# A hybrid encoder block on one core: the triangular inverses of two groups of heads computed together on 128 lanes, their operands brought to lanes through DRAM, and the filler work laid out anew

## The chip, the cores and the metric

The kernel runs on one core of a Trainium2 chip. The core has TensorE (PE, matrix products, results in PSUM), VectorE (DVE), ScalarE (ACT), GpSimd (POOL) and SyncE (SP), each working through its own list of instructions in order, and 16 DMA engines that all queues share. In this kernel SP issues the loads of weights and POOL nearly all other transfers. The metric is the device time of one execution in microseconds; a version's figure is the median of several executions.

## What is computed

The reference is one layer of a streaming encoder: 512 tokens, width 1024, everything float32. After an RMS norm one wide projection feeds three token mixers (a short gated convolution, a gated linear recurrence, and RWKV-7 time mixing), which are gated and summed; an output projection, a second norm, a squared-ReLU MLP with 4096 hidden units and a last norm follow. The part that matters here is the RWKV-7 mixing, with 16 heads of width 64:

```python
def step(state, inp):
    r_t, w_t, k_t, v_t, kk_t, a_t = inp
    sa = einsum('bhvk,bhk->bhv', state, -kk_t)
    state = (state * w_t[:, :, None, :]
             + sa[..., None] * (kk_t * a_t)[:, :, None, :]
             + v_t[..., None] * k_t[:, :, None, :])
    y_t = einsum('bhvk,bhk->bhv', state, r_t)
```

The kernel doesn't step through tokens. It takes chunks of 64 tokens (8 chunks). Inside a chunk the dependence of tokens on earlier ones is a strictly upper triangular 64x64 matrix A for each head and chunk, and (1 - A) has to be inverted: 16 heads x 8 chunks = 128 inverses of 64x64. Each is made of two 32x32 diagonal blocks, inverted by substitution, and of one off-diagonal block, which is a product of three 32x32 matrices: the first inverse, A's off-diagonal block, the second inverse.

## The kernel before

**Projections.** All large matrix products run in three passes: a float32 weight is loaded by SP (`raw`, two buffers), split into a high and a low half (`whi` by ScalarE in line 146, `wlo` by VectorE through the helper of line 103; three buffers each), and lines 167 to 169 multiply high x high, high x low and low x high. One projection (`proj`, line 306) is one weight of 128x1024, 8 slices x 3 matmuls, into one of three PSUM banks (`pp`); it yields after every second slice, so in four pieces. A bank is free again when ScalarE or VectorE has copied it out.

**Groups.** The 16 heads are four groups of four. For each group g:

- `krv(g)` (line 418) projects keys, receptances and values of the group and forms with many VectorE operations the scaled operands AR and BK. It has 26 yields (20 for group 0).
- `amat(g)` (line 517) multiplies them to the matrices A (and others) for all eight chunks, masks them into the tile AX (tag AXt, one buffer) in lines 529 and 530, and stores parts of it (axd) and the transposed BK (bkd) in DRAM for later. Three yields.
- `inverse(g)` (line 546) inverts the group's 32 matrices. Each of the 64 diagonal 32x32 blocks gets a lane of its own: two VectorE transposes (line 553) bring the blocks from AX to `la` in lanes 64 to 127 of the tile Z, identities come from an input `eyes` into `xt`, and 31 steps of substitution follow, two VectorE operations each (lines 562 and 567, both recorded under line 103), on 64 lanes. Two transposes (line 575) bring the result back to matrix form TT, a third (line 580) makes a transposed copy d1 of the first blocks. Then 32 matmuls pG (line 587), a ScalarE copy, 32 matmuls pT (line 597) and another copy make the off-diagonal blocks, reading AX itself as one operand. One DMA stores the finished TT in DRAM (ttd, line 600).

**Chain.** When all inverses are there, `chain` (line 628) goes through the eight chunks with the state carried from one to the next: each chunk loads its pieces of vtd, axd, ttd, rtd and bkd (line 608, all on POOL's queue) and runs four rounds of small matmuls. Layer output, MLP and the final norm follow.

**What sets the order.** The work is written as Python generators. `ab(q)` (line 744), for eight q, is the work of the other two mixers: seven projections and some 30 vector operations, in 29 yields; all eight in a row are the filler `fl`, 232 yields. `weave(crit, fill, r, base)` (line 823) advances the critical generator and gives the filler r steps for each of its yields; what the critical one issues goes into the planner with a priority offset (the value that it yielded, or `base`). The planner orders each engine's list by priority; `pin` (line 171) keeps small matmuls together, and `keep_in_program_order` keeps an instruction where it was written. The outer order is in lines 859 to 866:

```python
    weave(krv(0, GS[0]), fl, R0)
    for g in range(NG):
        if g:
            fgr = fill_group(g)
            weave(inverse(g - 1, GS[g - 1]), fgr, R1, CPV)
            drain(fgr)
        weave(amat(g, GS[g]), fl, 1.0)
    weave(inverse(NG - 1, GS[NG - 1]), fl, R2, CPV)
```

`fill_group(g)` (line 842) is itself a mix: F_INV = 30 filler steps, then `krv(g)` with F_KRV = 9 filler steps for each N_KRV = 22 of its yields, then F_GAP = 3. So an inverse of one group is woven with filler and with the next group's krv. N_TT = 2 and NINV = 12 are the empty yields in `inverse` around the transposes and between d1 and pG: they only let filler in. An inverse has 59 yields. Beside the chain the rest of the filler runs, then `gate(q)` (line 726) for eight q, then the first part of the output projection (`fill_chain`, line 880, at R3 = 1.6 steps for each yield of the chain).

Of the kernel before, what the change touches and what calls it, by code (L numbers as in the profile page):

```python
# [9 lines left out]
F32 = mybir.dt.float32  # L10
# [14 lines left out]
N_TT, NINV, NG_T, N_LOAD = 2, 12, 4, 6  # L25


N_KRV = 22
F_INV, F_KRV, F_GAP = 30, 9, 3
# [68 lines left out]
def block_kernel(ctx, tc, xt, win, par, mulr, sw, wout, w1, w2, fg, cst, eyes, out):  # L98
# [418 lines left out]
    def amat(g, G_):  # L517

        G_.AX = p1.tile([P, 2, NC, 4, L], F32, tag="AXt", name="AXt")
        for c4 in range(2):  # L520
# [10 lines left out]
            yield  # L531
        gp.dma_start(axd[:, 0:64, g, 1].rearrange("c s e t -> s c (e t)"),
# [13 lines left out]
    def inverse(g, G_):  # L546
        AXt = G_.AX
        Z = p1.tile([P, 2, 32, 32], F32, tag="Z", name="Z")
        la, xt = Z[64:128, 0], Z[64:128, 1]
        dg = p1.tile([P, 32, 32], F32, tag="dg", name="dg")  # L550
        tmp = dg[64:128].rearrange("p a b -> p (a b)")
        for b in range(2):
            v.transpose(la[32 * b:32 * b + 32].rearrange("l s t -> l t s"),
                        AXt[32 * b:32 * b + 32, 0, :, :, 32 * b:32 * b + 32].rearrange("s c e t -> s t (c e)"))
        gp.dma_start(xt.rearrange("l s t -> l (s t)"), eyes)

        yield
        yield
# [10 lines left out]
        TT = Z[0:64].rearrange("p a b c -> p (a b c)").rearrange("p (l t) -> p l t", t=L)  # L569
        gp.memset(TT[32:64, :, 0:32], 0.0)  # L570
        for b in range(2):
            for _ in range(N_TT):
                yield CPI
            tc.keep_in_program_order(
                v.transpose(TT[32 * b:32 * b + 32, :, 32 * b:32 * b + 32].rearrange("s l t -> s t l"),
                            xt[32 * b:32 * b + 32].rearrange("l s t -> l t s")))
# [3 lines left out]
        tc.keep_in_program_order(v.transpose(d1[0:32], TT[0:32, :, 0:32]))  # L580
        for _ in range(NINV):
            yield CPI
        for half in range(2):
            pg = pm.tile([P, 16, 32], F32, tag="pm", name="pG")
            for i in range(16):
                l = 16 * half + i
                pin(i, lambda: pe.matmul(pg[32:64, i], AXt[0:32, 0, l // 4, l % 4, 32:64], d1[0:32, l],  # L587
                                             start=True, stop=True))
            ac.copy(gs[32:64, 16 * half:16 * half + 16], pg[32:64])
# [3 lines left out]
        for half in range(2):  # L593
            pg = pm.tile([P, 16, 32], F32, tag="pm", name="pT")
            for i in range(16):
                l = 16 * half + i
                pin(i + half, lambda: pe.matmul(pg[0:32, i], gs[32:64, l], TT[32:64, l, 32:64], start=True, stop=True))
            ac.copy(TT[0:32, 16 * half:16 * half + 16, 32:64], pg[0:32])
# [9 lines left out]
    def load_chunk(c):  # L608
# [9 lines left out]
        gp.dma_start(flat(tc_), flat(ttd[c]))  # L618
# [223 lines left out]
    def fill_group(g):  # L842

        for _ in range(F_INV):
            next(fl, None)
            yield
        acc = 0.0
        for _ in krv(g, GS[g]):
            yield
            acc += F_KRV / N_KRV  # L850
# [4 lines left out]
        for _ in range(F_GAP):  # L855
# [275 lines left out]
```

## Time and profile before

| | us |
|---|---|
| median of 3 executions | 1103.43 (1099.84 to 1107.11) |
| the profiled execution | 1100.19 |
| its span, first to last instruction | 1098.4 |
| PE busy | 1053.0 (96%) |
| DVE busy | 735.3 (67%) |
| ACT busy | 486.4 (44%) |
| POOL busy | 93.7 (9%) |

The four amat stages begin at about 87, 204, 327 and 450 us; the chain's first matmuls run at 564 us, its last at 669 us; the MLP takes the time from about 750 us to the end. In the profile a line such as L103 or L106 is that of a helper, so groups of one kind are told apart by the names of tiles and by shape (dg and Z for the inverse's steps). "Idle before" is the time that an engine stood still ahead of an instruction, with the instruction that ended it. The granted clock is the share of its full rate at which TensorE ran.

### The profile page before, as it was taken

The page shows a single profiled execution, that of the slowest core. Times are in us where ns is not written, and L with a number is a line of the kernel's source. Part 1 is how long each engine was busy: PE and PEld are TensorE (multiplying, and loading weights), DVE is VectorE, ACT ScalarE, POOL GpSimd, SP SyncE. Part 2 cuts the span into 40 slices and gives each one's busy share as a digit, 9 for nine tenths or more (in the row PEclk, how much of TensorE's full clock was granted, in tenths as well). Part 3 has the DMA queues.
Part 4 walks back from the last instruction along what each step waited for, and adds up shares of the span by engine and source line. Part 5 has one row for each costly group of instructions (what it writes and reads, how often), then busy time and mean ns, then how long its engine had stood idle before and what let it go on. Part 6 is the DMA issues. An engine that isn't in the chain of part 4 may idle for free.

```text
span 1098.4 us, 16103 instructions
## 1 busy us (share of the span) xinstructions
PE 1053.0 (96%) x6396; PEld 863.2 (79%) x6396; DVE 735.3 (67%) x1266; ACT 486.4 (44%) x718; POOL 93.7 (9%) x159
## 2 busy tenths in 40 slices
PE   8999989999999979999699998999999999999996
PEld 5777867787877867788578886998888888888885
DVE  7998987899788987889547777855444443222224
ACT  7755455444573545363445444334444443111114
POOL 0011001110111002200031210101000000000001
PEclk9999989999999989999799999999999999999999
DMA  6336324452446224453288753334332335333232
GB/s 219 120 95 183 100 81 131 130 158 87 138 127 172 82 85 123 123 159 105 70 265 256 252 196 104 116 111 158 96 96 96 96 96 192 96 96 96 95 97 76
DMA packets 43323, 142.13 MB, mean 129 GB/s; under 512 B 5680, under 2 KB 9264, under 8 KB 42224
## 3 DMA queue, kind: packets, MB, share of 16 engines
q1 hardware_dynamic: 29472, 91.02, 25.9%
q0 software_dynamic: 13056, 49.03, 14.8%
q8 instruction: 50, 0.82, 0.3%
q10 hardware_dynamic: 720, 1.05, 0.3%
q14 instruction: 25, 0.20, 0.1%
HBM read 115.91 MB, written 25.17 MB: 128 GB/s over the span
## 4 chain that ended last, share of the span: by engine, by line
PE 47%; DVE 2%; ACT 1%; issue 1%; DMA 0%; DVEq 0%; ACTq 0%
PE acc L167 7%; PE acc L168 7%; PE acc L169 7%; PE p L168 5%; PE p L169 5%; PE p L167 5%; PE pp L167 2%; PE pp L169 2%; PE pp L168 2%; PE py L654 1%; PE pu L644 1%; PE pu L664 1%; PE pS L673 1%; PE pG L587 0%; DVE xr L106 0%
## 5 line engine op out<-in xcount | busy, mean ns | idle before, releaser
L103 DVE TENSOR_TENSOR wlo<-raw,whi 128x1024 fp32r<-128x1024 f32 (+1 forms) x164 | 197.9, 1208 | 228.5 <-ACT whi L146 222.7
L146 ACT CAST whi<-raw 128x1024 fp32r<-128x1024 f32 (+1 forms) x164 | 169.6, 1035 | 274.7 <-PE acc L169 125.0
L167 PE MATMUL pp<-hh,whi 128*128 128x512 f32 x688 | 275.1, 400 | 7.2 <-ACT g L799 4.2
L169 PE MATMUL pp<-hh,wlo 128*128 128x512 f32 x688 | 273.4, 397 | 2.7 <-DVE wlo L103 2.7
L168 PE MATMUL pp<-hl,whi 128*128 128x512 f32 x688 | 273.6, 398 | 0.0
L167 PEld LDWEIGHTS pp<-hh,whi 128*128 128x128 f32 x688 | 131.2, 191 | 37.0 <-ACT g L799 4.8
L169 PEld LDWEIGHTS pp<-hh,wlo 128*128 128x128 f32 x688 | 131.2, 191 | 32.3 <-DVE wlo L103 4.8
L168 PEld LDWEIGHTS pp<-hl,whi 128*128 128x128 f32 x688 | 131.3, 191 | 27.0
L167 PE MATMUL p<-h2h,whi 128*128 128x512 f32 (+1 forms) x264 | 101.4, 384 | 0.0
L168 PE MATMUL p<-h2l,whi 128*128 128x512 f32 (+1 forms) x264 | 101.2, 383 | 0.0
L169 PE MATMUL p<-h2h,wlo 128*128 128x512 f32 (+1 forms) x264 | 101.1, 383 | 0.0
L167 PE MATMUL acc<-whi,ah 128*128 128x512 f32 x256 | 99.6, 389 | 0.0
L168 PE MATMUL acc<-wlo,ah 128*128 128x512 f32 x256 | 99.6, 389 | 0.0
L169 PE MATMUL acc<-whi,al 128*128 128x512 f32 x256 | 99.6, 389 | 0.0
L167 PEld LDWEIGHTS p<-h2h,whi 128*128 128x128 f32 x264 | 49.6, 188 | 9.7
L168 PEld LDWEIGHTS p<-h2l,whi 128*128 128x128 f32 x264 | 49.7, 188 | 9.5
L169 PEld LDWEIGHTS p<-h2h,wlo 128*128 128x128 f32 x264 | 49.6, 188 | 9.6
L169 PEld LDWEIGHTS acc<-whi,al 128*128 128x128 f32 x256 | 48.0, 188 | 10.1
L167 PEld LDWEIGHTS acc<-whi,ah 128*128 128x128 f32 x256 | 48.0, 188 | 10.0
L168 PEld LDWEIGHTS acc<-wlo,ah 128*128 128x128 f32 x256 | 48.0, 188 | 9.9
L103 DVE TENSOR_TENSOR dg<-Z 64x31 f32<-64x31 f32 (+15 forms) x124 | 42.2, 340 | 4.1
L103 DVE TENSOR_TENSOR Z<-Z,dg 64x31 f32<-64x31 f32 (+15 forms) x124 | 42.2, 340 | 4.1
(304 smaller groups left out, 1465.7 us busy)
## 6 DMA issues: line engine op xcount, KB each, us to landing
raw<-in_win SPq DMA_DIRECT2D x88, 512.0 KB, 3.5
raw<-in_w SPq DMA_DIRECT2D x64, 512.0 KB, 3.5
ax<-axd POOLq DMA_DIRECT2D x8, 1024.0 KB, 7.5
axd<-AXt POOLq DMA_DIRECT2D x12, 512.0 KB, 7.1
bkd<-BKT POOLq DMA_DIRECT2D x4, 1024.0 KB, 12.4
raw<-in_wout SPq DMA_DIRECT2D x8, 512.0 KB, 3.6
bk<-bkd POOLq DMA_DIRECT2D x7, 512.0 KB, 8.5
swr<-in_sw SPq DMA_DIRECT2D x16, 128.0 KB, 2.3
```

The lines of the kernel that those rows point to most:

```text
L103: return v.tensor_tensor(out=o, in0=a, in1=b, op=op)
L146: ac.copy(hi[:, sl], raw[:, sl])
L167: pe.matmul(ps, wh, xh, start=start, stop=False)
L168: pe.matmul(ps, wh, xl, start=False, stop=False)
L169: pe.matmul(ps, wl, xh, start=False, stop=stop)
L644: pin(n, lambda: pe.matmul(pu[64 * h:64 * h + 64, x], ax[rows, g, 0, e], sv[rows, g, e], start=True, stop=True))
L654: pin(behind, lambda: pe.matmul(py[64 * h:64 * h + 64, x], w, y, start=first and x == 0, stop=last, skip_group_check=True))
L664: pin(n, lambda: pe.matmul(pu[64 * h:64 * h + 64, x], tc_[:, g, e], u0[:, g, e], start=True, stop=True))
L673: pin(n, lambda: pe.matmul(pS[64 * h:64 * h + 64, x], bk[:, x, 64 * h:64 * h + 64], sv[:, g, e], start=True, stop=True))
```

## The change

Groups 0 and 1 are inverted together, and groups 2 and 3. The 128 diagonal blocks of a pair fill 128 lanes, and the 31 steps run twice in the kernel, not four times. Lanes 64 b + 32 gi and on hold block b of group gi of the pair. Since a VectorE transpose can't bring the rows of two groups there, `amat` stores the diagonal blocks with two DMAs and the off-diagonal blocks with a third into DRAM buffers (`lad`, `odd`, one of each for a pair), from AX, on POOL's queue ahead of its other stores; `inverse` loads `la` from `lad` with one DMA. AX is no longer read by `inverse`. After the steps one transpose on all lanes makes TT (in the place of `la`), one more makes d1, and the off-diagonal blocks `od` are loaded over `xt`. The finished blocks are stored into ttd by four DMAs for the diagonal and two for the off-diagonal; ttd has its axes in another order, and the zero blocks are written once by four DMAs after the first krv. The pG and pT matmuls of the two groups alternate between two blocks of 32 lanes.

The order changes too: inverse(0) is woven with fill_group(2), inverse(1) with the filler after the last amat; groups 1 and 3 have no inverse beside them. The empty yields are now N_LA = 8 (new, ahead of the steps), N_TT = 1 at two places, NINV = 24; a pair's inverse has 73 yields.

```diff
-N_TT, NINV, NG_T, N_LOAD = 2, 12, 4, 6
+N_LA, N_TT, NINV, NG_T, N_LOAD = 8, 1, 24, 4, 6
-F_INV, F_KRV, F_GAP = 30, 9, 3
+FILL = {1: (4, 13, 5), 2: (36, 13, 5), 3: (4, 13, 5)}
...
-    ttd = dp.tile([NC, L, NG, 4, L], F32, name="ttd")
+    ttd = dp.tile([L, NG, NC * 4, L], F32, name="ttd")
+    lad = [dp.tile([P, 32, 32], F32, name=f"lad{p_}") for p_ in range(2)]
+    odd = [dp.tile([L, 32, 32], F32, name=f"odd{p_}") for p_ in range(2)]
...
+        gi, pr = g % 2, g // 2
+        ax = G_.AX[:, 0].rearrange("s c e t -> s (c e) t")
+        for b in range(2):
+            r = 64 * b + 32 * gi
+            gp.dma_start(lad[pr][r:r + 32].rearrange("l s t -> s l t"),
+                         ax[32 * b:32 * b + 32, :, 32 * b:32 * b + 32])
+        gp.dma_start(odd[pr][32 * gi:32 * gi + 32], ax[0:32, :, 32:64])
...
-    def inverse(g, G_):
-        AXt = G_.AX
+    def inverse(pr):
         Z = p1.tile([P, 2, 32, 32], F32, tag="Z", name="Z")
-        la, xt = Z[64:128, 0], Z[64:128, 1]
+        la, xt = Z[:, 0], Z[:, 1]
...
-        for b in range(2):
-            v.transpose(la[32 * b:32 * b + 32].rearrange("l s t -> l t s"),
-                        AXt[32 * b:32 * b + 32, 0, :, :, 32 * b:32 * b + 32].rearrange("s c e t -> s t (c e)"))
         gp.dma_start(xt.rearrange("l s t -> l (s t)"), eyes)
+        gp.dma_start(la.rearrange("l s t -> l (s t)"), lad[pr].rearrange("l s t -> l (s t)"))
+        for _ in range(N_LA):
+            yield
         for s in range(31):
...
-            mm = tt(tv, la[:, s, s + 1:32].unsqueeze(1).to_broadcast([64, c, n]),
-                    xt[:, 0:c, s:s + 1].to_broadcast([64, c, n]), MUL)
+            mm = tt(tv, la[:, s, s + 1:32].unsqueeze(1).to_broadcast([P, c, n]),
+                    xt[:, 0:c, s:s + 1].to_broadcast([P, c, n]), MUL)
...
-        for b in range(2):
-            for _ in range(N_TT):
-                yield CPI
-            tc.keep_in_program_order(
-                v.transpose(TT[32 * b:32 * b + 32, :, 32 * b:32 * b + 32].rearrange("s l t -> s t l"),
-                            xt[32 * b:32 * b + 32].rearrange("l s t -> l t s")))
+        for _ in range(N_TT):
+            yield CPI
+        TT, od = la, xt[0:64]
+        tc.keep_in_program_order(v.transpose(TT.rearrange("s l t -> s t l"), xt.rearrange("l s t -> l t s")))
+        gp.dma_start(od.rearrange("s l t -> s (l t)"), odd[pr].rearrange("s l t -> s (l t)"))
...
-        tc.keep_in_program_order(v.transpose(d1[0:32], TT[0:32, :, 0:32]))
+        tc.keep_in_program_order(v.transpose(d1[0:64], TT[0:64]))
+        for gi in range(2):
+            for b in range(2):
+                r, t = 64 * b + 32 * gi, slice(32 * b, 32 * b + 32)
+                gp.dma_start(ttd[t, 2 * pr + gi, :, t], TT[r:r + 32])
...
-            for i in range(16):
-                l = 16 * half + i
-                pin(i, lambda: pe.matmul(pg[32:64, i], AXt[0:32, 0, l // 4, l % 4, 32:64], d1[0:32, l],
-                                             start=True, stop=True))
-            ac.copy(gs[32:64, 16 * half:16 * half + 16], pg[32:64])
+            for n in range(32):
+                i, gi = n // 2, n % 2
+                l, r, o = 16 * half + i, slice(32 * gi, 32 * gi + 32), slice(64 + 32 * gi, 96 + 32 * gi)
+                pin(n, lambda: pe.matmul(pg[o, i], od[r, l], d1[r, l], start=True, stop=True))
+            ac.copy(gs[64:128, 16 * half:16 * half + 16], pg[64:128])
...
-        gp.dma_start(ttd[:, :, g].rearrange("c t e x -> t c (e x)"),
-                     TT.rearrange("t (c e) x -> t c (e x)", c=NC))
+        for gi in range(2):
+            gp.dma_start(ttd[0:32, 2 * pr + gi, :, 32:64], od[32 * gi:32 * gi + 32])
...
     def fill_group(g):
-        for _ in range(F_INV):
+        lead, among, gap = FILL[g]
+        for _ in range(lead):
...
+    for g in range(NG):
+        gp.dma_start(ttd[32:64, g, :, 0:32], zer[0:32, 0:32].unsqueeze(1).to_broadcast([32, NC * 4, 32]))
     for g in range(NG):
         if g:
             fgr = fill_group(g)
-            weave(inverse(g - 1, GS[g - 1]), fgr, R1, CPV)
+            if g == 2:
+                weave(inverse(0), fgr, R1, CPV)
             drain(fgr)
         weave(amat(g, GS[g]), fl, 1.0)
-    weave(inverse(NG - 1, GS[NG - 1]), fl, R2, CPV)
+    weave(inverse(1), fl, R2, CPV)
```

The pT matmuls change in the same way as pG, the loads of a chunk follow the new axes of ttd, and `eyes` has 128 rows where it had 64.

More of the change, by code (lines that the diff above doesn't have):

```diff
@@ L594, in inverse @@
             pg = pm.tile([P, 16, 32], F32, tag="pm", name="pT")
[L595 to L598, printed above, removed]
+            for n in range(32):
+                i, gi = n // 2, n % 2
+                l, r, o = 16 * half + i, slice(32 * gi, 32 * gi + 32), slice(64 + 32 * gi, 96 + 32 * gi)
+                pin(n + half, lambda: pe.matmul(pg[r, i], gs[o, l], TT[o, l], start=True, stop=True))
+            ac.copy(od[:, 16 * half:16 * half + 16], pg[0:64])
             yield
-        gp.dma_start(ttd[:, :, g].rearrange("c t e x -> t c (e x)"),
-                     TT.rearrange("t (c e) x -> t c (e x)", c=NC))
+        for gi in range(2):
+            gp.dma_start(ttd[0:32, 2 * pr + gi, :, 32:64], od[32 * gi:32 * gi + 32])
     C = {"St": None, "c": 0}
@@ L617, in load_chunk @@
         gp.dma_start(flat(ax), flat(axd[c]))
-        gp.dma_start(flat(tc_), flat(ttd[c]))
+        gp.dma_start(tc_.rearrange("s g e t -> s g (e t)"),
+                     ttd[:, :, 4 * c:4 * c + 4].rearrange("s g e t -> s g (e t)"))
         if c > 0:
@@ L849, in fill_group @@
             yield
-            acc += F_KRV / N_KRV
+            acc += among / N_KRV
             while acc >= 1.0:
@@ L854, in fill_group @@
                 yield
-        for _ in range(F_GAP):
+        for _ in range(gap):
             next(fl, None)
```

8 lines of the change are left out of this document (2 added, 6 removed).

## The prediction

> **What bounds the kernel now.** I read the page first: busy time of each engine and the span in 40 slices.
>
> ```profile
> PE 1053.0 (96%) x6396; PEld 863.2 (79%) x6396; DVE 735.3 (67%) x1266; ACT 486.4 (44%) x718; POOL 93.7 (9%) x159
> DVE  7998987899788987889547777855444443222224
> PEclk9999989999999989999799999999999999999999
> ```
>
> TensorE (PE) sets the time: 1053.0 us busy of a span of 1098.4. What can be won is the 45 us in which it is idle, and the time in which it is busy at a reduced clock. VectorE (DVE) is busy at 67% over the span, but at 8 or 9 tenths in the first 20 slices (to about 550 us), where the projections, the amat stages and the four inverses are woven. So I cut that stretch into windows of 10 us and looked for those where PE did less than full work.
>
> The rows below are us, then busy time (count) of PE, PEld, DVE, ACT, POOL, then the granted clock, DMA share and GB/s. The first is an undisturbed window for comparison, the last one (50 us long) the end of the chain.
>
> ```profile
> 110.00:120.00 10.00, 10.00 (x46) 8.29 (x45) 9.45 (x20) 5.38 (x6) 0.00 (x0) 1.00 0.37 109
> 140.00:150.00 10.00, 7.09 (x32) 5.53 (x30) 9.48 (x17) 2.20 (x3) 0.00 (x0) 1.00 0.20 66
> 150.00:160.00 10.00, 8.71 (x24) 6.53 (x25) 9.36 (x14) 5.86 (x8) 0.00 (x0) 0.66 0.17 52
> 160.00:170.00 10.00, 9.46 (x91) 7.67 (x90) 4.54 (x6) 7.81 (x12) 0.00 (x0) 0.90 0.33 108
> 170.00:180.00 10.00, 10.00 (x94) 7.91 (x94) 8.59 (x22) 5.38 (x9) 1.49 (x2) 0.93 0.35 93
> 260.00:270.00 10.00, 9.12 (x41) 7.23 (x40) 9.28 (x23) 1.26 (x3) 0.57 (x1) 1.00 0.37 131
> 270.00:280.00 10.00, 8.78 (x39) 6.93 (x38) 8.93 (x7) 3.46 (x6) 0.00 (x0) 1.00 0.26 61
> 400.00:410.00 10.00, 4.91 (x41) 3.55 (x40) 6.67 (x8) 7.03 (x10) 0.00 (x0) 0.67 0.29 107
> 410.00:420.00 10.00, 10.00 (x89) 7.68 (x89) 6.15 (x15) 4.53 (x8) 1.47 (x2) 0.81 0.26 86
> 520.00:530.00 10.00, 6.64 (x30) 5.17 (x28) 9.73 (x12) 5.60 (x8) 0.00 (x0) 0.99 0.32 104
> 530.00:540.00 10.00, 4.14 (x66) 4.01 (x67) 5.78 (x8) 3.61 (x7) 0.00 (x0) 0.50 0.20 52
> 540.00:550.00 10.00, 10.00 (x91) 7.89 (x90) 3.15 (x4) 4.71 (x8) 0.56 (x1) 0.83 0.25 80
> 650.00:700.00 50.00, 45.54 (x432) 38.89 (x431) 42.13 (x105) 20.06 (x39) 5.05 (x8) 0.97 0.34 116
> ```
>
> A full window does 46 matmuls of 128x512, 0.217 us each. What a window lost is its length less busy time times clock: in 150:160 that is 10 - 8.71 x 0.66 = 4.25 us (24 matmuls where 46 would fit says the same, 4.8). By this rule the four disturbed places lost 2.91 + 4.25 + 1.49 + 0.70 = 9.4 us, 0.88 + 1.22 = 2.1 us, 6.71 + 1.90 = 8.6 us and 3.43 + 7.93 + 1.70 = 13.1 us: together **33.1 us**. A longer gap costs twice, since the clock after it is 0.50 to 0.67; the short gaps at 260:280 cost no clock.
>
> The timeline (start, us, engine, instruction, then the idle time ahead of it and who ended that) shows that these four places are the four inverses' ends; here are the first, third and fourth.
>
> ```profile
> 145.38 4.00 DVE L575 STREAM_TRANSPOSE Z<-Z 32x1024 f32<-32x1024 f32 x2
> 150.13 0.63 ACT L785 ACTIVATE u<-u 128x512 f32<-128x512 f32 x1 [3.73 <-DVE u L103]
> 151.29 0.79 PE L167 MATMUL pp<-hh,whi 128*128 128x512 f32 x1 [4.20 <-ACT g L799]
> 402.90 0.51 PE L167 MATMUL pp<-hh,whi 128*128 128x512 f32 x1 [2.60 <-DVE ks L106]
> 407.84 1.91 PE L587 MATMUL pG<-dg,AXt 32*32 32x32 f32 x32 [2.49 <-ACT a L442]
> 534.49 1.23 DVE L580 STREAM_TRANSPOSE dg<-Z 32x1024 f32<-32x1024 f32 x1
> 535.86 3.59 PE L587 MATMUL pG<-dg,AXt 32*32 32x32 f32 x64 [9.22 <-DVE dg L580]
> ```
>
> First end: two transposes hold DVE for 4.00 us, ScalarE waits 3.73 us for a filler operation behind them, its copy of a projection's PSUM bank (L799) comes late, and PE waits 4.20 us for the bank. Third: the shift that frees a bank (ks) is late behind the same transposes. Fourth: the pG matmuls have their place in PE's order, and the transpose that feeds them (L580) runs 9.22 us too late, behind fillers on a DVE that lags.
>
> **The change, part by part.** *VectorE work.* The rows are group, shape, count | busy us, mean ns | idle before.
>
> ```profile
> L103 DVE TENSOR_TENSOR dg<-Z 64x31 f32<-64x31 f32 (+15 forms) x124 | 42.2, 340 | 4.1
> L103 DVE TENSOR_TENSOR Z<-Z,dg 64x31 f32<-64x31 f32 (+15 forms) x124 | 42.2, 340 | 4.1
> L553 DVE STREAM_TRANSPOSE Z<-AXt 32x1024 f32<-32x1024 f32 x8 | 16.8, 2099 | 0.2
> L575 DVE STREAM_TRANSPOSE Z<-Z 32x1024 f32<-32x1024 f32 x8 | 16.5, 2069 | 0.2
> L580 DVE STREAM_TRANSPOSE dg<-Z 32x1024 f32<-32x1024 f32 x4 | 4.9, 1229 | 0.1
> L665 DVE COPY sv<-pu 64x512 f32<-64x512 f32 x8 | 5.4, 679 | 2.4 <-PE pu L664 2.2
> L943 DVE COPY st<-tp 128x512 f32<-128x512 f32 x8 | 5.5, 688 | 5.0 <-DMA x2d<-st 4.5 <-PE tp L940 0.5
> ```
>
> Four times 62 steps become twice 62. A step on 128 lanes should cost what it costs on 64: copies of 512 elements take 679 ns on 64 lanes and 688 on 128. That saves (42.2 + 42.2) / 2 = 42.2 us. The transposes fall from 16.8 + 16.5 + 4.9 = 38.2 us to two strided ones of 2.07 and two of 1.23, 6.6 us: 31.6 us less. Together 74 us of DVE are gone from a stretch where it was the full engine. That is no gain in itself; it counts as far as PE's losses vanish.
>
> *The ends.* Four become two. At each the unbroken hold on DVE falls from 4.0 + 1.23 us to 2.07 + 1.23, with a filler step between. NINV goes from 12 to 24 yields, so at the last end some 20 filler steps instead of 10 stand between the small transpose and pG. A step is a quarter of a projection, 6 x 0.217 = 1.3 us of PE; the cover grows by 13 us, against a lateness of 9.22. So I take for each end that is left the smallest loss seen, 2.1 us; its bounds are 0 and the worst end's 13.1. Term: -33.1 + 2 x 2.1 = **-28.9 us**.
>
> *Rows to lanes through DRAM.* The rows are a DMA's operands, queue, count, KB each and median us to landing; the two q0 rows are packets, MB and share of 16 engines, first over the whole span, then in 64 to 80 us, when four DMAs with rows of 256 B (three axd<-AR, one rtd<-AR) ran in q0.
>
> ```profile
> axd<-AR POOLq DMA_DIRECT2D x16, 128.0 KB, 2.8
> bkd<-BKT POOLq DMA_DIRECT2D x4, 1024.0 KB, 12.4
> rtd<-AR POOLq DMA_DIRECT2D x8, 256.0 KB, 3.2
> q0 software_dynamic: 13056, 49.03, 14.8%
> q0 software_dynamic: 176, 0.52, 15.1%
> 94.32 2.48 DVE L103 TENSOR_TENSOR AXt<-pA,mask 128x512 f32<-128x512 f32 x4
> 99.34 0.90 POOL L543 DMA_DIRECT2D bkd<-BKT  x1
> 101.70 0.19 DVE L103 TENSOR_TENSOR dg<-Z 64x31 f32<-64x31 f32 x1
> ```
>
> New are 28 DMAs of 128 KB in rows of 128 B: three a group out of AX, six a pair into ttd, four of zeros. Rows of 256 B moved 0.52 MB in 15.1% of 16 us, 215 GB/s, where the queue's mean is 49.03 MB in 14.8% of 1098.4 us, 302 GB/s. If a row of 128 B costs what one of 256 B does, a DMA is 1.2 us of the 16 engines, all of them 34 us spread over 500: hidden behind a queue whose windows above stand at shares of 0.17 to 0.37. The chain's first load of tc waits for the last pair's two ttd stores, 256 KB where one of 512 KB stood: no later. POOL issues 26 DMAs more than before (34 new, 8 gone) at up to 0.9 us each; it is 9% busy, and behind them wait only stores and a memset for the next krv. I take nothing for any of these.
>
> The wait for la is another matter. AX is ready at 94.32 + 2.48 = 96.8 us, and DVE took its first step at 101.70. Now the load of la stands on POOL's queue behind three new stores, the axd stores and bkd, which landed at 99.34 + 12.4 = 111.7, 15 us after AX. With 3.6 us for the stores and some 2 us for its own 512 KB (at the mean rate), la lands about 21 us after AX. The first step then holds DVE's queue: the wlo halves of weights and the shifts that free PSUM stand behind it. Cover: N_LA = 8 yields at 0.8 make 6.4 filler steps, 8.3 us; three weight buffers hold 3 x 24 x 0.217 = 15.6 us more. 24 us against 21: just covered. I take 1.5 us of PE time for each pair, +3 us; bounds 0 and the rival below.
>
> The Trainium skill ("DMA: Bandwidth & Descriptors", Specifications) puts the least transfer for full rate at 512 B, with a read-modify-write below it; the 215 GB/s against 302 agree in sign.
>
> *Small matmuls.* As many as before (2 pairs x 2 halves x 32 = 4 groups x 2 x 16), same shapes, but alternating between two row blocks. Nearest row: L587 itself. I take 0; if neighbours ran side by side, half the 16 bursts would go. A burst of 32 instructions takes half of 3.59 us, but at half clock (window 530:540), so 0.9 at full: at most -7 us.
>
> *Filler.* By the code a q of ab() has 29 yields, 232 in all. Before the chain ran 17 + 3 x 43 + 12 + 50 = 208 of them; now 17 + (24 + 56 + 24) + 12 + 62 = 195. Thirteen steps, 17 us of PE work, move past the start of the chain: no change in PE's sum. They help at the chain's end, where PE lost 50 - 45.54 = 4.5 us waiting for the last norms and gates; bounds 0 and -4.5, I take -2. Groups 1 and 3 have no inverse any more, and more filler in each krv (13 per 22 yields, not 9), so krv's own waits are no barer than before.
>
> **Sum:** -28.9 + 3 - 2 = -27.9 us. The profiled execution took 1100.19 us (span 1098.4); 1072.3 is left. It lies 3.2 us below the median of 1103.43, so I say **1076 us**.
>
> **Rivals.**
> *Ends as dear as before.* The ends' waits come from the fixed order (a PSUM bank, ScalarE's queue), not from DVE's load; two ends at the mean of 8.3 us: 16.6 - 4.2 = 12.4 more, 1088 us. For it: the third end waited for ACT a (2.49 us) too. Against: each of those chains begins with a late DVE.
> *La late: the slower side.* One mechanism: DVE's queue stands at the first step until la lands, and everything later than 24 us after AX comes off PE, twice. If a 128 B row cost a whole mean packet (14.8% x 1098.4 x 16 / 13056 = 0.199 us), the three stores' 3072 rows would take 3072 x 0.199 / 16 = 38 us and la would land at 15 + 38 + 2 = 55: 31 us each, 1076 - 3 + 62 = 1135 us. It is slower than before from 39 us after AX on. Against it: 0.52 MB in rows of 256 B are 2000 rows in 176 packets, so a row is far less than a packet. In between, at 8 us a store, la lands at 15 + 24 + 2 = 41: 17 us each, 1076 - 3 + 34 = 1107 us, about no change.
> The Trainium skill ("VectorE: DVE Perf Modes", The three transpose paths) warns that a plain DMA which transposes by its access pattern is 19 times slower than the hardware's transposing path when the innermost destination stride is large; here the innermost 32 elements stay together, and no run here shows which holds. By that rule a store would be an estimated 19 x 0.43 = 8.2 us (128 KB at 302 GB/s, times 19), and the time the 1107 of the case in between.
> *The change doesn't do what it says.* Steps on 128 lanes cost twice: 42 us of DVE return and the ends stay as late, near 1100 us. The two COPY rows speak against it.
>
> **How the numbers follow.** About 1% (11 us) is what a measurement of this kernel can tell from no change. Chances: forecast 0.60; ends as dear 0.14; la late 0.17 (0.07 near no change, 0.10 slower); no relief 0.05, same; 0.04 for waits not seen here, slower. Of the forecast's 0.60 I put 0.02 within 1%, of the dear ends' 0.14 0.02. Faster 0.70, same 0.16, slower 0.14. The likeliest case's own range: 1076 - 4.2 - 3 - 2.5 - 7 = 1059, to 1088 with dear ends. With the la cases near no change the range is 1060 to 1108.
>
> **What would show it.** Right: L103 steps on dg and Z halved in count at 340 ns; DVE's tenths below 9 up to 500 us; at two ends PE waits under 3 us and a clock of 1.00; la landing within 24 us of AX. Wrong: PE idle right behind each pair's amat with DVE's first step waiting for a DMA (la late); a wait of over 3 us of PE for L580's successor or for a PSUM bank (ends dear); steps near 500 ns and more (no relief).

## The result, and the profile after

The changed kernel takes 1052.72 us (median of 4 executions, 1052.0 to 1054.87); the kernel before, in the same job, 1105.27 (4 executions, 1099.84 to 1109.47). The ratio is 0.953, interval 0.9484 to 0.9577. In a later job it was measured again: 1054.57, ratio 0.9545 (0.9531 to 0.9559). Forecast were 1076 us and a range from 1060 to 1108: the direction was right, the size was not. The profiled execution took 1053.11 us with a span of 1051.3, 47.1 us less than the one before; the other 5 us of the medians' 52.6 are there because the kernel before mostly runs at 1103 to 1105 and its profiled execution was a quick one.

The page of the changed kernel: busy time, the same slices as before, and the queue that POOL issues to.

```profile
PE 1027.3 (98%) x6396; PEld 845.4 (80%) x6396; DVE 651.6 (62%) x1126; ACT 482.5 (46%) x710; POOL 111.2 (11%) x181
DVE  6997596699864975994667678554444442212224
PEclk9999999999999999999999999999999999999999
q0 software_dynamic: 14240, 52.18, 17.4%
```

DVE is 83.7 us less busy, and its tenths, a row of 7 to 9 before (but for a 5 in the twentieth slice), stand at 4 to 7 in eleven of the first 20 slices. In the other nine they are still at 8 or 9, so one of the prediction's signs, tenths below 9 up to 500 us, didn't come. PE's busy time fell too, 1053.0 to 1027.3, with as many instructions: it now runs at its full clock (a mean of 0.996 where it was 0.979), and some instructions became cheaper (below). POOL's queue takes 17.4% of 1051.3, 183 us of the 16 engines, where it took 14.8% of 1098.4, 163: 20 us more, inside the 34 that the forecast hid beside other work.

The groups of DVE's steps and transposes (busy us, mean ns | idle before; in the second view min/median/max ns, first and last start):

```profile
L103 DVE TENSOR_TENSOR Z<-Z,dg 128x31 f32<-128x31 f32 (+15 forms) x62 | 21.1, 341 | 1.4
L103 DVE TENSOR_TENSOR dg<-Z 128x31 f32<-128x31 f32 (+15 forms) x62 | 21.1, 340 | 1.2
```

```profile
L580 DVE STREAM_TRANSPOSE Z<-Z x2: 2210/2220/2229, 246.5 to 460.9; 128x1024 f32<-128x1024 f32 x2
L585 DVE STREAM_TRANSPOSE dg<-Z x2: 1232/1240/1247, 249.2 to 464.1; 64x1024 f32<-64x1024 f32 x2
```

A step on 128 lanes costs what it cost on 64 (340 ns), and half of them are left: 42.2 us less. The transposes are 6.9 us where they were 38.2. That is 73.5, as forecast (74); that the engine's busy time fell by 10 more is no work saved, since the groups of all DVE instructions together fall by 73.9 (773.2 to 699.3): more of them overlap with their neighbour.

The two ends of the pairs, in windows of 10 us (columns as in the prediction), then the chain's end:

```profile
250.00:260.00 10.00, 10.00 (x163) 8.19 (x162) 9.42 (x22) 8.27 (x13) 4.29 (x6) 1.00 0.80 223
260.00:270.00 10.00, 10.00 (x162) 8.05 (x161) 7.83 (x13) 4.52 (x7) 1.54 (x4) 1.00 0.40 108
470.00:480.00 10.00, 10.00 (x164) 8.29 (x163) 3.05 (x3) 4.97 (x8) 0.00 (x0) 1.00 0.34 112
480.00:490.00 10.00, 10.00 (x162) 8.07 (x161) 4.73 (x8) 8.64 (x14) 1.56 (x2) 1.00 0.31 87
630.00:640.00 10.00, 6.74 (x35) 5.18 (x34) 7.30 (x18) 4.07 (x8) 0.86 (x2) 1.00 0.53 154
640.00:650.00 10.00, 10.00 (x72) 9.96 (x73) 9.40 (x28) 3.15 (x9) 2.52 (x4) 0.83 0.65 212
```

By the prediction's rule (length less busy time times clock) the ends of the inverses lose 0.00 us where four of them lost 33.1; PE waits for nothing there, and the clock is 1.00. The chain's end loses 3.26 + 1.70 = 5.0.

PE's waits over the whole span (total, times, longest) begin with this one, at the start; no row of over 1.2 us names a pG, a pp bank or a transpose's successor any more.

```profile
PE pst L273 <- DVE sq L103: 3.7, 1, 3.7
```

The way of la, first pair, in the timeline (start, us, engine, instruction [idle before <- by whom]), and the landing times of the new DMAs (count, KB each, median us):

```profile
179.88 2.48 DVE L103 TENSOR_TENSOR AXt<-pA,mask 128x512 f32<-128x512 f32 x4
182.83 1.61 POOL L539 DMA_DIRECT2D lad<-AXt  x2 [11.71 <-DVE AXt L103]
188.55 0.91 POOL L553 DMA_DIRECT2D bkd<-BKT  x1 [1.02 <-ACT u L796]
189.46 0.57 POOL L563 DMA_DIRECT2D Z<-lad  x1
208.32 0.18 DVE L103 TENSOR_TENSOR dg<-Z 128x31 f32<-128x31 f32 x1
```

```profile
axd<-AR POOLq DMA_DIRECT2D x16, 128.0 KB, 2.9
lad<-AXt POOLq DMA_DIRECT2D x8, 128.0 KB, 3.1
Z<-lad POOLq DMA_DIRECT2D x2, 512.0 KB, 13.7
Z<-odd POOLq DMA_DIRECT2D x2, 256.0 KB, 3.4
```

AX is ready at 182.4. The load of la, issued at 189.5, lands 12.9 us later (14.5 in the second pair; the row has the median), at 202.4: 20.0 us after AX, and 20.6 in the second pair (forecast about 21). The first step runs at 208.3 without any idle time ahead of it. A store in rows of 128 B out of AX lands in 3.1 us (lad) or 3.8 (odd), one out of Z into ttd in 4.0, and one of the same size in rows of 256 B in 2.9. The Trainium skill ("VectorE: DVE Perf Modes", The three transpose paths) warns of a factor of 19 for a plain DMA copy that transposes by its access pattern, where the innermost destination stride is large; here, where 32 elements stay together, these 3.1 to 4.0 us, against the 8.2 that the prediction worked out from it, show no such factor.

The prediction has no term for a second new wait. The off-diagonal blocks od, which pG reads, go over xt, so their load (Z<-odd) can be issued only when the first transpose has read xt:

```profile
249.03 0.54 POOL L581 DMA_DIRECT2D Z<-odd  x1 [41.71 <-DVE Z L580]
```

It lands 3.2 us later at the first end, at 252.3, and 3.6 us later at the second, at 466.9. In the changed kernel pG stands over 5 us behind both landings (257.4 and 472.5), so nothing waits for it; e3 and e5 show what it costs with fewer yields ahead of pG.

The small matmuls of the pairs' ends, in the timeline, now as x128 or x64 in one row (each float32 matmul of the program is two instructions there):

```profile
257.44 2.21 PE L597 MATMUL pG<-dg,Z 32*32 32x32 f32 x128
265.02 1.20 PE L607 MATMUL pT<-Z,dg 32*32 32x32 f32 x64
```

Before, an undisturbed pG was this (same columns):

```profile
282.89 1.19 PE L587 MATMUL pG<-dg,AXt 32*32 32x32 f32 x32
```

32 took 1.19 us, 37 ns each; now 128 take 2.21, 17 ns each. The forecast had left it as a bound.

**Where the 47.1 us are.** I summed, for each target of a matmul, the time from its start to the start of the next matmul. pp (the projections) fell from 538.9 to 507.1 us, pG and pT from 20.4 to 8.8, pA and pb (which ran at reduced clock behind the ends) from 26.8 to 21.3; the start rose by 2.0, the rest is under 1 us each. Cut the other way:

| where | us |
|---|---|
| the ends of the inverses (windows: 33.1 to 0.0) | -33.1 |
| small matmuls (17.3 at full clock group by group, as e1 measures below, to 8.8) | -8.5 |
| the chain's end (680:690 before, 5.35, to 4.96) | -0.4 |
| the start (this one execution; 0.3 in the second measurement) | +2.0 |
| left over, in krv and amat | -7.1 |

By the prediction's rule, summed in windows of 10 us over the whole span, PE's loss fell from 59.9 to 26.1 us. Of these 33.8 the table's ends, chain and start are 31.5, so of the 7.1 left over only some 2 us are waits and reduced clock (330:340 before, around the third amat, lost 2.75). For the other 5 PE was busy at its granted clock; what made that shorter stays open.

### The profile page after: what moved, and what is told of

It reads as the page before. It is cut to its first block, busy times and chain, and to the rows that moved or that the text cites. A ratio compares the mean times of both kernels' runs of the same rounds, so it can differ in the third digit from the quotient of the medians.

```text
span 1051.3 us, 15991 instructions
## 1 busy us (share of the span) xinstructions
PE 1027.3 (98%) x6396; PEld 845.4 (80%) x6396; DVE 651.6 (62%) x1126; ACT 482.5 (46%) x710; POOL 111.2 (11%) x181
## 3 DMA queue, kind: packets, MB, share of 16 engines
q0 software_dynamic: 14240, 52.18, 17.4%
## 5 line engine op out<-in xcount | busy, mean ns | idle before, releaser
L167 PE MATMUL pp<-hh,whi 128*128 128x512 f32 x688 | 270.7, 394 | 0.4 <-DVE rs L106 0.4
L168 PE MATMUL pp<-hl,whi 128*128 128x512 f32 x688 | 270.3, 393 | 0.0
L169 PE MATMUL pp<-hh,wlo 128*128 128x512 f32 x688 | 269.0, 391 | 0.2 <-DVE wlo L103 0.2
L1016 ACT CAST ah<-r 128x512 fp32r<-128x512 f32 x32 | 19.9, 622 | 43.4 <-DVE r L103 43.4
L167 PE MATMUL acc<-mh,whi 128*128 128x256 f32 x128 | 35.0, 288 | 1.5 <-ACT mh L733 1.5
```

Of the source, the lines that this page charges most:

```text
L167: pe.matmul(ps, wh, xh, start=start, stop=False)
L168: pe.matmul(ps, wh, xl, start=False, stop=False)
L169: pe.matmul(ps, wl, xh, start=False, stop=stop)
L1016: ac.copy(ahi, r)
```

## The experiments

Three questions: are the small matmuls the unforeseen term (theory A: neighbours on different blocks of lanes run side by side; the rival: they cost what they did); and is it the load that DVE lost (theory L) or the new places of the empty yields and filler (theory O) that empties the ends; and was a wait for la close. Differences are against 1052.7 (against the second measurement they are 1.9 us less).

| kernel | median us | ratio to before (interval) |
|---|---|---|
| e1_by_group | 1062.34 | 0.9609 (0.9575 to 0.9643) |
| e2_before_yields | 1085.12 | 0.9823 (0.9798 to 0.9848) |
| e3_after_old_yields | 1063.11 | 0.9622 (0.9597 to 0.9646) |
| e4_double_steps | 1083.81 | 0.981 (0.9774 to 0.9846) |
| e5_no_nla | 1063.44 | 0.9637 (0.9597 to 0.9676) |
| e6_old_fill | 1074.10 | 0.9721 (0.9686 to 0.9756) |
| e7_two_halves | 1055.86 | 0.9556 (0.9521 to 0.959) |
| e8_before_cover | 1100.23 | 0.9953 (0.9936 to 0.997) |
| e9_fin_early | 1049.99 | 0.9506 (0.9473 to 0.9538) |
| e10_even_fill | 1065.66 | 0.964 (0.9614 to 0.9666) |
| e11_after_again | 1054.57 | 0.9545 (0.9531 to 0.9559) |
| e12_fin_again | 1049.24 | 0.9496 (0.9482 to 0.951) |

The kernel before stood at 1103.96 (e1 to e4), 1103.17 (e5 to e7, e9) and 1104.96 (e8, e10 to e12).

### e1: the small matmuls group by group

In both loops:

```diff
-                i, gi = n // 2, n % 2
+                i, gi = n % 16, n // 16
```

> The changed kernel with its pG and pT matmuls in another order: the 16 of the first group, then the 16 of the second, so that neighbours read the same 32 lanes. Theory A (neighbours on different lanes of the array run side by side): the 512 small matmul instructions, which take 4.3 + 4.5 us in the changed kernel, take twice as long as in the kernel before at full clock, 17.3 us, and the time rises by 8 to 9 us to about 1061. Rival (the saving in these matmuls came from the clock alone): they stay at 17 ns each and the time at 1053, within 2 us.

The timeline's small matmuls:

```profile
255.88 4.70 PE L597 MATMUL pG<-dg,Z 32*32 32x32 f32 x128
268.23 2.11 PE L607 MATMUL pT<-Z,dg 32*32 32x32 f32 x64
```

The same 128 take 4.70 us, not 2.21; start to start, pG and pT together take 9.1 + 8.2 = 17.3 us, not 8.8. Theory A holds: only the alternation of the two groups makes them cheaper. The Trainium skill ("TensorEngine Tiling (Array Packing)", Key Properties) says that different tiles of the array can load weights and multiply in parallel; these rows agree, with a factor of 2.0 for two blocks.

The 8.5 us aren't all of it. Behind the two long runs of pG the granted clock falls, though PE waits for nothing there:

```profile
260.00:270.00 10.00, 10.00 (x93) 8.09 (x92) 5.74 (x8) 2.32 (x3) 1.45 (x3) 0.73 0.14 41
480.00:490.00 10.00, 10.00 (x73) 8.29 (x70) 1.29 (x2) 3.70 (x7) 0.00 (x0) 0.66 0.01 2
```

The projections take 5.0 us more for it (512.1 against 507.1). With a start that was 1.7 us shorter this time, that is about the 11.2 us by which the span of the profiled execution grew; the median rose by 9.6.

### e2: the kernel before with the new yields

```diff
-N_TT, NINV, NG_T, N_LOAD = 2, 12, 4, 6
+N_TT, NINV, NG_T, N_LOAD = 1, 24, 4, 6
```

> The kernel before with only the empty yields of the change around its transposes (N_TT 1, NINV 24 in place of 2 and 12). Theory L (DVE's load makes the ends late): the wait of 9.2 us of pG for the small transpose at the last end goes, the waits for PSUM banks at the ends stay; 5 to 13 us faster than before, 1092 to 1100. Rival O (the order alone makes them late): nearly all of the 33 us lost at the four ends goes, about 1072. Second rival: pG gets later, the waits for banks move with it, no change.

18.8 us faster: more than L allows, less than O. PE's waits:

```profile
PE pp L167 <- ACT g L799: 4.6, 2, 4.2
PE pp L169 <- DVE wlo L103: 4.6, 5, 1.2
PE pn L451 <- ACT a L442: 3.7, 2, 2.6
PE pp L167 <- DVE ks L106: 2.6, 1, 2.6
```

The wait of 9.2 us for pG at the fourth end is gone, and with it, in windows, 11 us of the 13 lost there; the first end (4.2 for ACT g) and the third (ks, ACT a) stand as they were. The spans of the two profiled executions differ by only 14.2 us, since that of the kernel before was a quick one. Twenty filler steps ahead of pG repair the fault for which they are the cover, and no other.

### e3: the changed kernel with the old yields

```diff
-N_LA, N_TT, NINV, NG_T, N_LOAD = 8, 1, 24, 4, 6
+N_LA, N_TT, NINV, NG_T, N_LOAD = 8, 2, 12, 4, 6
```

> The changed kernel with the old empty yields (N_TT 2, NINV 12; N_LA 8 kept). Theory L: with 74 us less DVE work the ends stay without losses, within 4 us of the changed kernel's 1053. Rival O: with half the filler between the small transpose and pG the last end waits as it did, 9 us and a slow clock after it, and the first pair's end some 5: 1063 to 1072.

10.4 us slower: the time that theory O gave, but not for its reason. The load of od, the small transpose and pG in the timeline:

```profile
248.38 0.54 POOL L581 DMA_DIRECT2D Z<-odd  x1 [42.17 <-DVE Z L580]
248.54 1.24 DVE L585 STREAM_TRANSPOSE dg<-Z 64x1024 f32<-64x1024 f32 x1
251.90 3.49 PE L597 MATMUL pG<-dg,Z 32*32 32x32 f32 x128 [2.88 <-DVE wlo L103]
472.64 2.72 PE L597 MATMUL pG<-dg,Z 32*32 32x32 f32 x128 [3.19 <-DVE u L106]
```

Both ends wait again, but not for DVE. Its small transpose is done at 249.78, and the operations that the rows name, wlo and u, are no operands of pG. The load of od lands 3.4 us after its issue, at 251.8 (3.6 us and 472.5 at the second end), and pG starts 0.1 us later both times. PE stood still from 249.02 and 469.45 on, and the small transposes were done at 249.78 and 470.82; so an estimate from these rows is that without od 0.8 and 1.4 us of waiting would be left. No wait for a PSUM bank came back. In the changed kernel, then, the new yields cover a load that the change itself brought in. In windows:

```profile
240.00:250.00 10.00, 9.02 (x40) 7.13 (x38) 9.73 (x20) 4.80 (x6) 1.56 (x3) 1.00 0.33 101
250.00:260.00 10.00, 8.10 (x141) 7.12 (x142) 4.04 (x5) 3.98 (x6) 2.73 (x4) 0.66 0.59 156
```

The wait of 2.88 us costs 0.98 + (10 - 8.10 x 0.66) = 5.6 us, since the clock behind it falls to 0.66; the second costs 5.4 in the same way (clock 0.70). Together they are 11.0, near the 10.4.

### e4: the load given back

The first operation of each step runs three times with the same values, 124 operations more.

```diff
+            for _ in range(2):
+                tt(tv, la[:, s, s + 1:32].unsqueeze(1).to_broadcast([P, c, n]),
+                   xt[:, 0:c, s:s + 1].to_broadcast([P, c, n]), MUL)
             tt(xt[:, 0:c, s + 1:32], xt[:, 0:c, s + 1:32], tv, ADD)
```

> The changed kernel with the first operation of each of the 31 steps issued three times instead of once (the same values again, nothing left out): 62 steps' worth of it, 2 x 21 us, so the 42 us of DVE work that the pairing saved are given back, at the same places in the order. Theory L: losses of PE come back at the two ends, 8 us each or more: 1065 to 1090. Rival O: the order is unchanged, so the time stays within 5 us of 1053.

31 us slower, though DVE's busy time is only 36.1 us up (687.7) and still 48 us under that of the kernel before. PE's waits:

```profile
PE pn L454 <- ACT a L445: 6.7, 2, 5.5
PE pG L600 <- issue: 4.7, 1, 4.7
PE pp L167 <- DVE ks L106: 3.4, 1, 3.4
PE pG L600 <- DMA Z<-odd: 1.3, 1, 1.3
```

These waits have three sources. DVE is late again: ks comes 3.4 us too late at the first end, and at the second the small transpose is done 2.2 us after PE stood still. pG then waits for od's load: 1.3 us at the first end, and the last 2.4 of the 4.7 at the second, where pG starts at 517.41 and od lands at 517.3. The longest wait, 5.5 us for ACT a at 356.9, is not DVE's. ScalarE had waited for a weight there, whose load was issued at 341.03 beside the stores of an amat and landed 12.1 us later, with the 16 DMA engines at a share of 0.95 (340:350); the next weight took 3.5 us:

```profile
353.21 1.04 ACT L146 CAST whi<-raw 128x1024 fp32r<-128x1024 f32 x1 [8.34 <-DMA raw<-in_win]
```

Nor was the order kept: the planner put about a tenth of DVE's other operations and of ScalarE's in other places than in the changed kernel. So the returned load does bring waits for DVE back, as L says, but how much of the 31 us it is by itself isn't separated here.

Put e2, e3 and the two kernels in a square: with the old yields the rest of the change (DVE's load, the filler, the way through DRAM) is worth 1104 - 1063 = 41 us, with the new ones 1085 - 1053 = 32, of which the small matmuls are 8.5 each time; the yields are worth 19 in the kernel before and 10 in the changed one. They don't cover the same thing: before it is a late DVE, now it is the load of od.

### e5: no yields ahead of the steps

`N_LA` is 0 where it was 8.

> The changed kernel with N_LA 0 in place of 8: no filler is let in between the load of la and the first step. The first step stood 26 us behind AX in the changed kernel, la landed 21 us behind it, so nothing waited. If the rule of the prediction holds (PE is covered for some 16 us by three weight buffers beyond the filler ahead of the step), the first step now stands some 5 to 10 us behind AX and DVE waits for la for 10 us or more; PE loses 0 to 5 us a pair: 1053 to 1063. Rival (weights' low halves go ahead of the step in DVE's order, so that a wait for la costs nothing): 1053, within 2 us. Second rival: DVE's stop empties PE, over 10 us a pair: above 1070.

10.7 us slower, and not by a wait for la. AX, the first step and the two pG in the timeline:

```profile
178.43 2.48 DVE L103 TENSOR_TENSOR AXt<-pA,mask 128x512 f32<-128x512 f32 x4
206.88 0.18 DVE L103 TENSOR_TENSOR dg<-Z 128x31 f32<-128x31 f32 x1
251.18 2.40 PE L597 MATMUL pG<-dg,Z 32*32 32x32 f32 x128 [2.95 <-DVE g L106]
470.96 3.32 PE L597 MATMUL pG<-dg,Z 32*32 32x32 f32 x128 [3.31 <-DVE u L106]
```

The first step stands at 206.88 - 180.91 = 26.0 us after AX, as in the changed kernel (208.32 - 182.36 = 26.0), and again waits for nothing. These yields don't decide when the steps begin; they only let 6 filler steps more in ahead of pG, and without them pG waits as in e3: od, issued at 247.60 and 467.43, lands at 251.1 and 470.9, 0.1 us ahead of pG each time. That the planner puts the first step behind its own estimate of the landing would fit both; it wasn't tried. The prediction's reading of N_LA as la's cover falls.

### e6 and e10: other layouts of the filler

```diff
-FILL = {1: (4, 13, 5), 2: (36, 13, 5), 3: (4, 13, 5)}
+FILL = {1: (30, 9, 3), 2: (30, 9, 3), 3: (30, 9, 3)}
```

for e6, the numbers of before for every group; for e10 three times (22, 9, 3).

> The changed kernel with the old amounts of filler in each of the three groups (30 ahead, 9 for 22 yields, 3 after), 220 filler steps ahead of the chain where there are 195. Theory L (what counts is DVE's load and the cover of pG): the ends stay without losses, only krv in groups 2 to 4 has less filler; 1053 to 1060, the chain's end perhaps 3 us dearer. Rival O (the layout of filler is what made the gain): 15 us or more are lost, 1068 and above.

> The changed kernel with nearly as much filler ahead of the chain (35 steps in each of the three groups, 105 together, where the change has 24, 56 and 24) but the same amount in each group. If the amount left for the chain is what the layout gives: within 5 us of the changed kernel's 1053, since the run with 129 steps lost most at the chain's end. If the split between groups counts (more filler beside the pair's inverse): 7 us or more dearer, lost at the first pair's end, where krv of group 2 stands ahead of pG.

e6 is 21.4 us slower. With 30 steps beside groups that have no inverse, 25 more are used up ahead of the chain, and the chain's end runs dry: in windows 640:680 loses 13.7 us, where the changed kernel's end lost 5.0. The rest is lost at the first pair's end (7.3, behind a wait for ks of the krv beside it) and at the chain's start (3.3). Among PE's waits:

```profile
PE pYt L725 <- DVE Y L103: 6.9, 1, 6.9
PE pp L167 <- DVE ks L106: 2.4, 1, 2.4
```

e10 uses up as much ahead of the chain as the change (3 x 35 steps, 104 there) and is still 11.1 us slower than the changed kernel in the same job (1065.66 against 1054.57): the fill_group beside inverse(0) has 35 steps where the change has 56, and PE loses 8.9 us there (260:290), behind a late bank and then od's load. Another 5.3 go at the chain's start (520:550), where it waits for DMAs. In the timeline:

```profile
267.69 0.80 PE L167 MATMUL pp<-hh,whi 128*128 128x512 f32 x1 [4.27 <-ACT g L824]
283.99 2.21 PE L597 MATMUL pG<-dg,Z 32*32 32x32 f32 x128 [1.63 <-DMA Z<-odd]
525.10 1.49 PE L655 MATMUL pu<-sv,ax 128*64 128x64 f32 x32 [2.00 <-DMA ax<-axd]
```

The layout of the filler, amount and place together, is thus worth 11 to 21 us by itself; the prediction took 2 for it.

### e7: the transpose in two halves

```diff
-        tc.keep_in_program_order(v.transpose(TT.rearrange("s l t -> s t l"), xt.rearrange("l s t -> l t s")))
+        for b in range(2):
+            hs = slice(64 * b, 64 * b + 64)
+            tc.keep_in_program_order(v.transpose(TT[hs].rearrange("s l t -> s t l"),
+                                                 xt[hs].rearrange("l s t -> l t s")))
```

> The changed kernel with the transpose behind the steps made in two halves of 64 lanes, one right behind the other, so that DVE is held for 4.2 us in one piece as in the kernel before (2.2 in the changed kernel). If that hold is what empties PE: 3 to 5 us lost at each of the two ends, 1059 to 1063. If the hold matters only where DVE is late already: 1053 to 1055.

```profile
244.73 4.48 DVE L582 STREAM_TRANSPOSE Z<-Z 64x1024 f32<-64x1024 f32 x2
```

At the first pair the two stand back to back and hold DVE for 4.48 us, longer than the 4.00 at the first end of before; at the second pair another operation comes between them. PE waits once behind the first end, 0.92 us for wlo, and not at the second. The median is 3.1 us above the changed kernel's first measurement and 1.3 above its second, with ratios whose intervals overlap; the span of the profiled execution is 0.4 down (1050.9). So the unbroken hold, which the prediction named at the first and the third end, costs PE under 1 us where DVE has room. That it costs more where DVE is late already would fit, but this run doesn't show it.

### e8: the kernel before with more cover

```diff
-N_TT, NINV, NG_T, N_LOAD = 2, 12, 4, 6
+N_TT, NINV, NG_T, N_LOAD = 1, 32, 4, 6
-F_INV, F_KRV, F_GAP = 30, 9, 3
+F_INV, F_KRV, F_GAP = 22, 9, 3
```

> The kernel before (an inverse for each group, all of its DVE work) with the order of the change as far as it goes: N_TT 1, NINV 32 (the sum of the change's 24 and 8 ahead of its steps), F_INV 22 in place of 30, so that some 199 filler steps run ahead of the chain, near the change's 195. Theory L (DVE's load keeps its own part of the loss): the first and third end keep their waits for PSUM banks, 8 to 10 us each, and the time stays at 1076 to 1087. Rival O (order and filler are all, beside the 8.7 us of the small matmuls): 1060 to 1068.

4.7 us faster than before, 15 slower than e2: worse than either theory said. PE's waits begin with:

```profile
PE pn L451 <- ACT a L442: 11.3, 4, 3.6
```

Banks behind the shifts ks (7.8 us in all) and rs (7.0) follow. No pG waits, but the waits sit in krv now, which runs beside the inverse with the lead of 22 steps. It looks as if at DVE's full load a longer cover in one place bared another. Two numbers were changed at once, so the run doesn't say which of them did it.

### e9, e11 and e12: a better version

The largest loss left is the chain's end, where `fin_m` (the gating products of the first four chunks) stands behind all gates. In e9 and e12, the same kernel, the four groups of `fin_m(0, 4)` come two gates behind their own:

```diff
+        fin = 0
         for q in range(KT):
             yield from gate(q)
+            while C["c"] >= 4 and 2 * fin + 1 <= q - 2:
+                yield from fin_m(0, 4, [fin])
+                fin += 1
...
-        yield from fin_m(0, 4)
+        yield from fin_m(0, 4, range(fin, NG))
```

> The changed kernel with the gating products of a pair of head groups (fin_m) set two gates behind the gates that feed them, not behind all eight gates. The changed kernel loses about 5 us at the chain's end, where PE waits for gc and ym of the last gates and its clock falls to 0.83. If those waits stand on the last gates being directly ahead of fin_m: 3 to 5 us faster, 1048 to 1050. Rival (DVE is the bound there, 6 to 9 tenths busy, and the waits move): 1053, within 2 us.

> The changed kernel once more, on the chip of the next run: 1053, within 2 us.

> The changed kernel with the gating products of a pair of head groups set two gates behind the gates that feed them, once more, beside the changed kernel on one chip: 3 to 5 us faster than that if the 4.6 us of TensorE's time that the profile showed won at the chain's end come through in full; no difference beyond 1 us if the earlier pair of runs differed by the chip alone.

1049.99 and, on one chip beside the changed kernel's 1054.57, 1049.24: 5.3 us faster, with intervals that don't meet (0.9482 to 0.951 against 0.9531 to 0.9559). The chain's end in windows of e12:

```profile
630.00:640.00 10.00, 9.56 (x49) 7.76 (x48) 7.39 (x17) 5.61 (x11) 1.07 (x2) 1.00 0.34 114
640.00:650.00 10.00, 10.00 (x84) 9.80 (x83) 9.54 (x27) 3.30 (x9) 2.83 (x4) 1.00 0.75 238
```

0.44 us are lost where it was 5.0. This is the fastest of all versions here.

## Why the prediction was wrong in size

The steps, in the order of the sum (us of the profiled execution):

| step | forecast | measured | shown by |
|---|---|---|---|
| ends of the inverses | -28.9 | -33.1 | windows |
| wait for la | +3 | 0 | timeline, e5 |
| load of od | no term | 0, since it is covered | timeline, e3, e5 |
| small matmuls | 0 | -8.5 | e1 |
| filler, chain's end | -2 | -0.4 | windows |
| start | 0 | +2.0 | one execution only |
| krv and amat | 0 | -7.1 | what is left over |
| sum | -27.9 | -47.1 | |

The remaining 4 us between 1076 and 1052.7 are the step from the profile to the median: the forecast added 3.2, the changed kernel's profiled execution lies 0.4 above its median.

- **What bounds the kernel, and the mechanism**: right. PE's losses sat at the inverses' ends, they followed a late DVE, and they went in a kernel with half of that load; with the old yields (e3) they stay away, and with the load given back (e4) DVE is late again. How much of it is the load and how much the new layout of the filler isn't separated: e6, with the load halved and the old layout, loses 7 us at the first pair's end.
- **DVE's saving**: right, 73.5 us against 74, with 340 ns for a step on 128 lanes; the rival that steps cost twice falls with it.
- **The ends' remaining loss**: for each end "the smallest loss seen, 2.1 us" was taken; it is 0. A loss seen under a full DVE is no floor for a DVE with 74 us less to do. The prediction counted the new yields as cover against a late DVE, whose wait had been 9.22 us. In the changed kernel they cover the landing of od, a load that the prediction left without a term and that costs 11 us where they are too few (e3, and e5 in the same way). That the kernel had room for it is luck as far as the forecast goes. e7 shows that the unbroken hold, on which its reading of two ends leaned, isn't a cause by itself.
- **The small matmuls**: the failed step. "I take 0" was the bound that the rows before favoured, since no row showed neighbours on different lane blocks. The other bound, -7, had been worked out and was the truth; it was short by 1.5 because a burst was put at 0.9 us by halving a row at a clock of 0.50, where e1 has 17.3 / 16 = 1.08 and an undisturbed row of the trace 1.19 with its last matmul's tail. The alternation also keeps the clock up, which no term foresaw (e1: 5.0 us).
- **The wait for la**: the landing was right to 1 us (20.0 and 20.6 against 21). That the first step would hold DVE's queue was wrong: its place in DVE's list is 26 us after AX, behind the landing, with N_LA = 8 and with 0. The slower rival, la late, needed stores of 8 us and more; they took 3.1 to 4.0.
- **The filler**: taken as 2 us, for the chain's end alone. e6 and e10 show 21 and 11 us for other layouts of the same filler, lost at the first pair's end and at both ends of the chain. Some of the 7.1 us of krv and amat may belong here or to the lower load; no run separates it.
- **The range**: its low end of 1060 came from adding the low bounds of the terms that were listed. The small matmuls went 1.5 us beyond their bound, and the 7.1 of krv and amat had no term: the prediction only says that krv's waits get no barer.

Still open: what made the 7.1 us of krv and amat, how the lower load of DVE and the layout of the filler divide the gain at the ends (e4 gave back operations of the steps only, and the order moved with them), and what e8 lost by which of its two numbers.

## What to carry to other kernels

When an engine that is nearly full is relieved, the losses that followed its lateness don't shrink to the smallest seen; they can vanish. A change that sends data through DRAM brings a wait of its own, which needs room in the in-order lists: here 3.4 us for od, worth 11 us where it was bare. The profile named other operations for that wait, which had nothing to do with it; compare what a wait is put down to with the operands, and with the landing of their loads. Cost the layout of the filler as a term of its own, in each stage where it is spent, and look at what is late in the stage next to it. When an edit alters which lanes neighbouring small matmuls use, price it by both bounds and ask which the hardware allows: here that was 8.5 us that no row of the trace before could show.

## What the runs showed of the hardware

- Matmul instructions of 32x32 float32 (two for a matmul of the program) on one block of lanes, in a row, take 34 ns each (17.3 us for 512 in e1), alternating between two blocks 17 ns (8.8 us for 512).
- A run of 128 such instructions on one block (4.70 us in e1) is followed by a granted clock of 0.73 and 0.66 in the next 10 us, though PE waits for nothing; with alternation (2.21 us) the clock stays at 1.00.
- A single wait of PE of about 3 us (2.88 and 3.19 in e3) cost 5.6 and 5.4 us, since the granted clock behind it fell to 0.66 and 0.70: a wait is priced with the clock that follows.
- A DMA of 128 KB from GpSimd's queue landed in 3.1 (lad), 3.8 (odd) and 4.0 us (ttd) in rows of 128 B, in 6.7 where it stored zeros, and in 2.9 us in rows of 256 B.
- A load of a weight issued beside the stores of an amat landed after 12.1 us, the next one after 3.5 (e4, issued at 341.03 and 355.54).
